# Hybrid decoder block on one core: attention weights scaled on GpSimd, compressed values in two heads at once, scan outputs parked in DRAM, one float32 product for each state

## The chip, the cores and the metric

The kernel runs on one core of a Trainium2 chip. Its engines are TensorE (PE: matmuls and transposes; PEld is its weight load), VectorE (DVE), ScalarE (ACT), GpSimd (POOL) and SyncE (SP, which issues all DMAs here). Each engine works through its own instructions in the order in which the program lists them and waits on semaphores for the others. The metric is device time in microseconds (us), median of several runs.

## The reference

One decoder layer over 1024 tokens of width 1024, in float32, cut here to what the change touches:

```python
h = rms_norm(x, norm1_w[l]) * (1.0 + sc1) + sh1
q, kv, nsa_g, z, xbc, dt_raw, mg = jnp.split(h @ w_in[l], IN_OFFSETS, axis=-1)
...
# sparse attention, 16 heads in 2 groups: compressed, selected and window branches
p_c = masked_softmax(s_c, cmp_end[None, :] <= t[:, None])      # 63 compressed keys
o_c = jnp.einsum('bgjtn,bngd->btgjd', p_c, v_cmp)
...
o = gb[..., 0:1] * o_c + gb[..., 1:2] * o_s + gb[..., 2:3] * o_w
...
# state-space scan, 4 groups of 8 heads, 8 chunks of 128 tokens in each
y_diag = jnp.einsum('bcgjls,bcsgjp->bclgjp', cb[:, :, :, None] * decay_in, xdt)
states = jnp.einsum('bcsgn,bcsgjp->bcgjpn', bm, xdt * decay_out[..., None])
y_off = jnp.einsum('bclgn,bcgjpn->bclgjp', cm, prev) * jnp.exp(a_cum)   # prev: state before the chunk
y = _rms(((y_diag + y_off) + d_skip * xs) * silu(z))             # by group
...
x = x + gt1 * ((g_attn * y_attn + g_ssm * y_ssm) @ w_o[l])
x = x + gt2 * ((silu(h2 @ w_gate[l]) * (h2 @ w_up[l])) @ w_down[l])
```

With 1024 tokens there are 16 blocks and 16 are selected, so the selected branch is causal attention over all keys.

## The kernel before

Most products are made of three: each float32 operand is split into a high part and the rest (`hi`, `lo`, in a format that TensorE takes at the rate of 512 columns in some 0.23 us), and hi·hi, hi·lo and lo·hi are added up (`mm3k`, lines 278 to 282). The split itself is ACT work (hi) and DVE or POOL work (lo; weights' lo is POOL's, L311).

The program is written out by a planner (`Flow`). Streams of TensorE work (Python generators) say what each step needs and how long it takes; four queues (A for ACT, V for DVE, G for POOL, D for DMA) hold the other work with a cost in us, which the planner multiplies by 1.15, 1.15, 1.2 and 1.0. It plays the streams against these costs and emits each instruction when it would start. So costs set the order in which each engine finds its work, and nothing else: on the chip each engine takes that order and waits where it must. Main streams go first; a filling stream (`background`) is put in where no main stream could go on, or as a credit allows that grows with `pace` times the main work.

Four stages follow each other. Projections (q, k, v, gates; the constants, cos and sin among them, lie in one tile `kc`). Attention: 32 units of 4 heads by 128 queries. For each of two branches, `score` makes S = qK (L1702), finds the row maximum on DVE (L1707), the exponential on ACT (L1711), and scales each head's P by 1/sum and its gate (L1720, DVE, four in a row). `value_step` turns P by 128 keys and 4 heads on TensorE (L1787), splits it (L1790 ACT, L1791 DVE) and `products` multiplies with V (L1018). The compressed branch has 64 keys: its turned P fills 64 partitions, and its two products have 64 rows. The filling stream here is the rest of the input projection (x, z and merge gates: `fps`), with the convolution on DVE (L1064, L1080), and `mod_rows` on POOL (L1276, L1279). Scan: 32 chunks; `prep` and `main` of `Chunk` make the diagonal part (yd), the part of the old state (yo), the norm and the new state (sp, st). In groups 0 and 1 yo and sp are single float32 products (L1922, L1949: two instructions each on TensorE); in groups 2 and 3 they are made in parts (`parts`, L1883 to L1888, and three products). `turn_y` turns each y for the output product, into tiles of the tag h32, of which there are three: two hold the attention's output until its product is done (`attn_done`), and one the first yT. The filling stream is the rest of the merge gates, the attention's output product (`aps`) and the scan's (`sps`). The last quarter of `sps` and the feed-forward layer are the tail, whose TensorE work stands without gaps.

## Time and profile before

| what | value |
|---|---|
| timed runs | 2707.79, 2699.96, 2702.74 us, median 2702.74 |
| the profiled execution | 2705.52 us, its span 2703.7 us |
| PE busy | 2581.8 us, 95% of the span |
| DVE, ACT, POOL busy | 1737.9, 1152.5, 664.0 us (64%, 43%, 25%) |
| mean granted TensorE clock | 0.977 |

A share of busy time is a mean over stages with different limits: PE is near full nearly everywhere, DVE is busiest in the attention and the scan, and nearly all of PE's idle time lies before the tail. The granted clock is given in shares of full speed (2.4 GHz); its lower level, 0.50, is 1.2 GHz. Times in a trace are counted from the span's start.

### The profile page before, as it was taken

How to read it: one execution, taken by the hardware profiler on the slowest of the kernel's cores; microseconds unless marked ns; L12 is line 12 of the kernel's file. 1: busy time of each engine (PE TensorE's matmuls, PEld its weight loads, DVE VectorE, ACT ScalarE, POOL GpSimd, SP SyncE). 2: the span in 40 equal slices, each digit the busy share in tenths (PEclk: the TensorE clock that was granted, in tenths of full speed). 3: DMA queues.
4: the chain of work that ended last, by engine and by line, in shares of the span. 5: the costliest groups of instructions: out<-in, count | busy, mean ns of one | idle time of the engine just before them, and what ended most of it. 6: DMA issues, size and time to landing. Idle time of an engine off the chain costs nothing.

```text
span 2703.7 us, 38173 instructions
## 1 busy us (share of the span) xinstructions
PE 2581.8 (95%) x14098; PEld 2185.0 (81%) x14098; DVE 1737.9 (64%) x4053; ACT 1152.5 (43%) x2458; POOL 664.0 (25%) x397
## 2 busy tenths in 40 slices
PE   6999999989998999999998999989999999999997
PEld 5999778878887888887877888769988888888885
DVE  7644987887886888877557579877722333333336
ACT  4322665556564655665545355542621111111113
POOL 2112222131222232312242322212122112222223
PEclk8999999999999999999998999989999999999999
DMA  6434232222223232212455544335221111111111
GB/s 234 142 105 143 85 86 63 64 78 71 63 67 126 86 92 73 90 43 71 138 164 190 188 139 129 106 122 171 73 77 40 39 47 47 47 47 47 47 55 63
DMA packets 206555, 253.95 MB, mean 94 GB/s; under 512 B 15256, under 2 KB 150040, under 8 KB 205856
## 3 DMA queue, kind: packets, MB, share of 16 engines
q1 hardware_dynamic: 206368, 251.51, 29.9%
q8 instruction: 111, 1.82, 0.3%
q14 instruction: 76, 0.62, 0.1%
HBM read 195.75 MB, written 55.71 MB: 93 GB/s over the span
## 4 chain that ended last, share of the span: by engine, by line
PE 79%; DVE 13%; DMA 3%; ACT 3%; issue 2%; SPq 0%; POOL 0%; DVEq 0%; ACTq 0%; POOLq 0%
PE fps L280 6%; PE gu L280 6%; PE fps L282 6%; PE fps L281 6%; PE gu L281 6%; PE gu L282 6%; PE o L1018 5%; PE tp L1787 4%; PE S L1702 4%; DVE P L1720 3%; PE dps L282 3%; PE dps L281 3%; PE dps L280 3%; PE yd L1905 2%; PE tokps L282 2%
## 5 line engine op out<-in xcount | busy, mean ns | idle before, releaser
L1569 DVE TENSOR_TENSOR x<-x,dps 128x512 f32<-128x512 f32 x176 | 120.9, 687 | 248.8 <-PE dps L282 248.6
L280 PE MATMUL gu<-m_hi,whi_w 128*128 128x512 f32 x704 | 279.8, 397 | 0.0
L281 PE MATMUL gu<-m_lo,whi_w 128*128 128x512 f32 x704 | 276.2, 392 | 0.0
L282 PE MATMUL gu<-m_hi,wlo_w 128*128 128x512 f32 x704 | 274.6, 390 | 0.0
L1790 ACT ACTIVATE kv<-tp 128x512 fp32r<-128x512 f32 (+1 forms) x296 | 172.9, 595 | 228.0 <-PE tp L1787 204.9
L311 POOL TENSOR_TENSOR wlo_w<-raw_w,whi_w 128x1024 fp32r<-128x1024 f32 x44 | 109.5, 2509 | 533.3 <-ACT whi_w L309 533.3
L1791 DVE TENSOR_TENSOR kv<-tp,kv 128x512 fp32r<-128x512 f32 (+1 forms) x296 | 196.7, 684 | 51.2 <-ACT kv L1790 50.0
L1018 PE MATMUL o<-kv 128*128 128x512 f32 x528 | 193.4, 420 | 12.5 <-DVE kv L1791 9.7
L1711 ACT ACTIVATE P<-P,sm 128x640 f32<-128x640 f32 (+7 forms) x256 | 186.5, 730 | 33.7 <-DVE sm L1707 32.4
L1702 PE MATMUL S<-kv,Q 128*128 128x384 f32 (+5 forms) x768 | 185.8, 344 | 6.7 <-DVE sm L1707 6.5
L1720 DVE TENSOR_SCALAR P<-P,sm,gate 128x640 f32<-128x640 f32 (+7 forms) x256 | 188.5, 800 | 1.2
L1787 PE MATMUL tp<-id,P 128*128 128x128 f32 x1056 | 157.9, 277 | 9.5 <-DVE Q L1666 5.9
L280 PE MATMUL fps<-hT_hi,whi_x 128*128 128x512 f32 x384 | 159.7, 416 | 4.0 <-ACT xs L1105 3.3
L282 PEld LDWEIGHTS gu<-m_hi,wlo_w 128*128 128x128 f32 x704 | 132.3, 188 | 33.0
L1787 PEld LDWEIGHTS tp<-id,P 128*128 128x128 f32 x1056 | 128.3, 142 | 37.5 <-issue 11.2
L280 PEld LDWEIGHTS gu<-m_hi,whi_w 128*128 128x128 f32 x704 | 132.1, 188 | 29.9
L281 PEld LDWEIGHTS gu<-m_lo,whi_w 128*128 128x128 f32 x704 | 131.8, 187 | 30.3
L282 PE MATMUL fps<-hT_hi,wlo_x 128*128 128x512 f32 x384 | 152.6, 397 | 0.0
L281 PE MATMUL fps<-hT_lo,whi_x 128*128 128x512 f32 x384 | 152.5, 397 | 0.0
L280 PE MATMUL fps<-whi_z,hT_hi 128*128 128x256 f32 x512 | 150.8, 295 | 0.9 <-ACT u L1067 0.6
L1702 PEld LDWEIGHTS S<-kv,Q 128*128 128x128 f32 x768 | 129.8, 194 | 24.0 <-DVE sm L1707 9.9
L1707 DVE CUSTOM_DVE_ANT_0 P<-S,kb 128x256 f32<-128x256 f32 (+5 forms) x256 | 120.5, 493 | 42.7 <-PE tp L1787 32.8
(342 smaller groups left out, 7046.7 us busy)
## 6 DMA issues: line engine op xcount, KB each, us to landing
wada<-w_ada SPq DMA_DIRECT2D x40, 512.0 KB, 4.3
ac<-acd SPq DMA_DIRECT2D x32, 512.0 KB, 4.9
raw_x<-w_in SPq DMA_DIRECT2D x24, 512.0 KB, 5.1
raw_w<-w_gate SPq DMA_DIRECT2D x22, 512.0 KB, 4.3
raw_w<-w_up SPq DMA_DIRECT2D x22, 512.0 KB, 3.8
rawd<-w_down SPq DMA_DIRECT2D x22, 512.0 KB, 3.8
xsd<-xs SPq DMA_DIRECT2D x32, 256.0 KB, 2.4
raw_z<-w_in SPq DMA_DIRECT2D x16, 512.0 KB, 4.7
```

Source lines behind the costliest of these rows:

```text
L280: mm(ps, lh, rh, start=k == 0, stop=False)
L281: mm(ps, lh, rl, start=False, stop=False)
L282: mm(ps, ll, rh, start=False, stop=k == kt - 1)
L1018: op = yield ([need, o], 0.22, lambda n=n, m=m, vst=vst, rows=rows, pair=pair: nc.tensor.matmul(o.t, vst(), pair()[m][:rows], start=n + m ...
L1569: e = V(0.6, [op], lambda ps=ps, t=t, cs=cs: nc.vector.tensor_tensor(self.x1[:, t, cs], self.x1[:, t, cs], ps.t, op=OP.add))
L1702: mm(sp[:, :w], q, kvb.kv[:, br, r, first + c0:first + c1], start=r == 0, stop=r == 1)
L1707: nc.vector.tensor_tensor_reduce(P[:, c0:c1], sp[:, :w], k.kb[:, m0:m0 + w], scale=-1.0, scalar=sm[:, 0, h:h + 1] if p else 3.0e38, op0=OP ...
L1711: ex = A(0.26 + 0.8333e-3 * n, [mx], lambda: nc.scalar.activation(P[:, :n], P[:, :n], AF.Exp, bias=sm[:, 1, h:h + 1], scale=-1.0, accum_ou ...
L1720: nc.vector.tensor_scalar(P[:, :n], P[:, :n], sm[:, 3, m:m + 1], k.gate[:, i, self.h0 + m, br + 1:br + 2], op0=OP.mult, op1=OP.mult)
L1787: nc.tensor.transpose(tp[:rows, h], P, k.id)
L1790: hi = A(0.48, [op, pair], lambda: nc.scalar.activation(pair()[0][:rows], tp[:rows], AF.Copy))
L1791: lo = V(0.6, [hi], lambda: nc.vector.tensor_sub(pair()[1][:rows], tp[:rows], pair()[0][:rows]))
```

## The change

Six things change.

- The scale of P (four for each branch of each unit, 256 in all) is issued on GpSimd instead of VectorE, with a cost of 0.25 + 1.08e-3 n.
- The compressed branch turns two heads at once (two transposes of 128 by 128 instead of four of 128 by 64), splits 128 by 256 instead of 64 by 512, and multiplies with values that stand twice, in the upper and the lower 64 partitions, with zeros between (`cvc`): four products of 128 rows and 256 columns instead of two of 64 rows and 512.
- In groups 2 and 3 of the scan the products with the state and for the state are single float32 ones as in groups 0 and 1; `parts` is gone.
- y of groups 1 and 2 is stored to DRAM by `main` and read back by `turn_y`; group 1 is not turned before `attn_done`.
- The pace of the scan's filling is 10 for 4.6 us of main work, in place of 16 in the first eight chunks and 5.6 after.
- The costs of the convolution are 2.5 and 0.75 instead of 2.25 and 0.66. cos, sin and one of the triangles move from `kc` to a tile `kt` in a buffer of the tag a1 that is given back after the projections.

```diff
@@ rope, load_constants, projections
-        cb = self.kc[:, K_COS + 8 * t:K_COS + 8 * t + 8][:, None, :].to_broadcast(sh)
+        cb = self.kt[:, 8 * t:8 * t + 8][:, None, :].to_broadcast(sh)
...
-        nc.sync.dma_start(self.kc, a["kc"][:, 0:K_ID])
+        nc.sync.dma_start(self.kc, a["kc"][:, 0:K_COS])
+        nc.sync.dma_start(self.kt.t, a["kc"][:, K_COS:K_ID])
...
+        self.kt = self.buf("a1", [128, K_ID - K_COS], "kt")
...
+        self.kt.until(*self.ktuse)
@@ products
-                vst, rows, pair, hi, lo = self.pv.pop(0)
-                for m, need in ((0, hi), (1, lo)):
-                    op = yield ([need, o], 0.22, lambda n=n, m=m, vst=vst, rows=rows, pair=pair: nc.tensor.matmul(
-                        o.t, vst(), pair()[m][:rows], start=n + m == 0, stop=n == u.total - 1 and m == 1))
+                vst, pair, hi, lo = self.pv.pop(0)
+                def product(m, n=n, vst=vst, pair=pair, o=o, u=u):
+                    if vst is None:
+                        for r in range(2):
+                            nc.tensor.matmul(o[:, r::2], self.cvc[:, u.g, r].rearrange("n r d -> n (r d)"),
+                                             pair()[m][:, 0:256], start=False, stop=False)
...
@@ background
-            c = V(2.25, [a0, a1, e], conv)
+            c = V(2.5, [a0, a1, e], conv)
...
-            f = V(0.66, [th], lambda: nc.vector.scalar_tensor_tensor(u.t, xr[:, 3:], 1.0, u.t, op0=OP.add, op1=OP.mult))
+            f = V(0.75, [th], lambda: nc.vector.scalar_tensor_tensor(u.t, xr[:, 3:], 1.0, u.t, op0=OP.add, op1=OP.mult))
@@ ssd, turn_y
-        pace = lambda: (16 if self.done < 8 else 5.6) / cost
+        pace = lambda: 10 / cost
...
-            while not self.ys:
+            while not self.ys or g == 1 and not self.attn_done:
                 yield None
             y, need = self.ys.pop(0)
+            if g in (1, 2):
+                y = self.buf("b", [128, 8, 64], f"yl{g}{c}")
+                need = D(0.73, [need, y], lambda y=y, g=g, c=c: nc.sync.dma_start(y.t.rearrange("p h d -> p (h d)"), self.yd[g - 1, c]))
@@ Unit.score
-                nc.vector.tensor_scalar(P[:, :n], P[:, :n], sm[:, 3, m:m + 1], k.gate[:, i, self.h0 + m, br + 1:br + 2],
+                nc.gpsimd.tensor_scalar(P[:, :n], P[:, :n], sm[:, 3, m:m + 1], k.gate[:, i, self.h0 + m, br + 1:br + 2],
                                         op0=OP.mult, op1=OP.mult)
-            self.P[br, m] = self.P[br, m][0], V(0.2 + 0.55e-3 * n, [e], scale)
+            self.P[br, m] = self.P[br, m][0], G(0.25 + 1.08e-3 * n, [e], scale)
@@ Unit.value_step
+        n = 2 if br == 2 else 4
+        c = slice(0, 128 * n)
...
+            for h in range(n):
+                P = self.P[2, 0][0][:, 2 * h:2 * h + 2].rearrange("p h n -> p (h n)") if br == 2 \
+                    else self.P[br, h][0][:, j * 128:(j + 1) * 128]
+                nc.tensor.transpose(tp[:, h * 128:h * 128 + 128], P, k.id)
@@ Chunk.main
-            if in_parts:
-                hi, lo, *es = self.parts("sp", lambda: self.bct[:, 1], self.l_bc, old, oldop)
...
+            op = yield ([oldop, yo], 0.86, lambda: nc.tensor.matmul(
+                fl(yo.t), self.bct[:, 1], fl(old.t), start=True, stop=True))
...
+        if self.g in (1, 2):
+            e = D(0.73, [e], lambda: nc.sync.dma_start(k.yd[self.g - 1, c], fl(y.t)))
+            y.until(e)
         k.ys.append((y, e))
```

Since the planner emits by costs, the order moves on every engine. Three places are shown. First DVE before, at the scale of the first branch of unit 2_0 of group 0 (P are its four heads, sm their sums; `ISA` is the row maximum):

```order
L1064 SCALAR_TENSOR_TENSOR u<-xr,hcw,u 128x512 x3
L1791 TENSOR_TENSOR kv_2828<-tp_1_1_3914,kv_2828 64x512
L1717 RECIPROCAL sm_2_0_3785<-sm_2_0_3785 128x4
L1665 TENSOR_TENSOR Q_2_1_3995<-tq_2_1_3960,Q_2_1_3995 64x256
L1666 TENSOR_TENSOR Q_2_1_3995<-tq_2_1_3960,Q_2_1_3995 64x256
L1080 SCALAR_TENSOR_TENSOR u<-xr,u 128x512
L1720 TENSOR_SCALAR P_2_0_3921<-P_2_0_3921,sm_2_0_3785,gate 128x384
L1720 TENSOR_SCALAR P_2_0_3949<-P_2_0_3949,sm_2_0_3785,gate 128x384
L1720 TENSOR_SCALAR P_2_0_3956<-P_2_0_3956,sm_2_0_3785,gate 128x384
L1720 TENSOR_SCALAR P_2_0_3968<-P_2_0_3968,sm_2_0_3785,gate 128x384
L1707 ISA P_2_0_4048,sm_2_0_3964<-S_2_0_3965,kb 128x384
```

And POOL now, at the same unit (wlo_x and wlo_z are weights' low parts for the filling, xr the convolution's input):

```order
L1762 TENSOR_SCALAR P_2_0_3793<-P_2_0_3793,sm_2_0_3718,gate 128x384
L1762 TENSOR_SCALAR P_2_0_3821<-P_2_0_3821,sm_2_0_3718,gate 128x384
L311 TENSOR_TENSOR wlo_x_3965<-raw_x_0_3907,whi_x_3939 128x1024
L1762 TENSOR_SCALAR P_2_0_3839<-P_2_0_3839,sm_2_0_3718,gate 128x384
L1762 TENSOR_SCALAR P_2_0_3849<-P_2_0_3849,sm_2_0_3718,gate 128x384
L311 TENSOR_TENSOR wlo_x_3965<-raw_x_4_3951,whi_x_3939 128x1024
L1108 MEMSET xr 128x3
L1762 TENSOR_SCALAR P_2_0_3953<-P_2_0_3953,sm_2_0_3852,gate 128x384
```

The four scales leave the row of convolution, splits and maxima on DVE and stand on POOL, in this unit with the low part of a weight tile between the second and the third.

Second, TensorE at the compressed step of the last unit, 7_1 of group 1 (Pc is its P, o the sum over keys, fps filling). Before:

```order
L1787 MATMUL tp_7_1_13668<-id,Pc_7_1_13519 64x128 x4
L280 MATMUL fps<-hT_hi,whi_m_13475 128x512
L281 MATMUL fps<-hT_lo,whi_m_13475 128x512
L282 MATMUL fps<-hT_hi,wlo_m_13491 128x512
L1018 MATMUL o_7_1_13557<-kv_8653 128x512
...
L1018 MATMUL o_7_1_13557<-kv_8653,cvc 128x512 x2
L1787 MATMUL tp_7_1_13687<-id,P_7_1_13450 128x128
```

Now:

```order
L1829 MATMUL tp_7_1_13672<-id,Pc_7_1_13518 128x128 x2
L1053 MATMUL o_7_1_13572<-kv_8506 128x512
...
L1050 MATMUL o_7_1_13572<-kv_8506,cvc 128x2x128 x2
L280 MATMUL fps<-hT_hi,whi_m_13516 128x512
L281 MATMUL fps<-hT_lo,whi_m_13516 128x512
L282 MATMUL fps<-hT_hi,wlo_m_13544 128x512
L1050 MATMUL o_7_1_13572<-kv_8506,cvc 128x2x128 x2
```

Two transposes stand where four stood, and two products of 256 columns for each one of 512. Over all 32 units the two products of before follow each other directly in 7 and are parted by other work in 25.

Third, TensorE where the scan ends. Before:

```order
L280 MATMUL yo_7_18199<-sph_7_18180 128x512
L281 MATMUL yo_7_18199<-spl_7_18190,sph_7_18180 128x512
L282 MATMUL yo_7_18199<-sph_7_18180,spl_7_18190 128x512
L1347 MATMUL yT_18216<-id,yy_6_18064 128x128 x4
L1347 MATMUL yT_18230<-id,yy_7_18183 128x128 x4
L280 MATMUL sps<-yT_17440,whi_so_17706 128x512
```

Now:

```order
L281 MATMUL sps<-yT_16986,whi_so_17450 128x512
L282 MATMUL sps<-yT_16986,wlo_so_17461 128x512
L1389 MATMUL yT_17837<-id,yy_7_17744 128x128 x4
L280 MATMUL sps<-yT_16986,whi_so_17450 128x512
```

Before, the last two y are turned side by side right after the last yo, and 96 rows of sps follow, the last quarter of them all, which needs those y. Now other sps stand on both sides, and 267 rows follow. Between the first and the last diagonal part there are 1371 rows of filling in the order before and 1179 now, each of 512 columns.

## Rows read from the trace of the kernel before

**Rows 1.** Busy time by stretch: attention, first part of the scan, its end, the tail. Columns: stretch and length in us, then PE, PEld, DVE, ACT, POOL busy (instructions), granted clock, DMA share, GB/s.

```profile
270.00:1335.00 1065.00, 1020.07 (x5959) 870.10 (x5958) 874.50 (x1952) 622.72 (x1435) 275.56 (x175) 0.98 0.26 79
1335.00:1493.00 158.00, 149.32 (x699) 119.83 (x698) 96.19 (x237) 78.43 (x167) 48.42 (x33) 0.96 0.58 184
...
1580.00:1830.00 250.00, 230.65 (x1130) 190.01 (x1130) 208.14 (x560) 135.83 (x320) 58.01 (x46) 0.93 0.39 121
1830.00:2704.00 874.00, 855.54 (x4088) 708.03 (x4086) 354.37 (x605) 191.16 (x289) 204.81 (x94) 1.00 0.20 62
```

**Rows 2.** Whom PE waited for in the attention, longest in total first: us in all, times, longest.

```profile
PE o L1018 <- DVE kv L1791: 10.0, 6, 5.6
PE S L1702 <- DVE sm L1707: 6.5, 4, 3.1
```

**Rows 3.** The longest of these waits: first the timeline of DVE, then of POOL, then of PE (start us, us, instruction, count, idle time before it), then the stretch behind the wait with its clock (columns as in rows 1).

```profile
596.68 5.77 DVE L1720 TENSOR_SCALAR P<-P,sm,gate 128x640 f32<-128x640 f32 x4
...
598.75 1.89 POOL L1276 TENSOR_TENSOR wada<-wada,sc 128x1024 f32<-128x1024 f32 x1 [0.83 <-DMA wada<-w_ada]
...
605.41 1.22 PE L1018 MATMUL o<-kv 128*128 128x512 f32 x2 [5.62 <-DVE kv L1791]
...
604.10:610.90 6.80, 5.49 (x20) 4.75 (x21) 5.49 (x13) 2.43 (x4) 4.34 (x4) 0.50 0.11 39
```

**Rows 4.** Costliest groups on DVE (from the page): busy us, mean ns of one.

```profile
L1720 DVE TENSOR_SCALAR P<-P,sm,gate 128x640 f32<-128x640 f32 (+7 forms) x256 | 188.5, 800 | 1.2
...
L1064 DVE SCALAR_TENSOR_TENSOR u<-xr,hcw,u 128x512 f32<-128x512 f32 x144 | 129.4, 898 | 11.7 <-ACT u L1067 7.9
```

**Rows 5.** Shortest, median and longest duration in ns of three DVE lines.

```profile
L1720 DVE TENSOR_SCALAR P<-P,sm,gate x256: 327/607/3009, 270.5 to 1307.8; 128x640 f32<-128x640 f32 x40, 128x128 f32<-128x128 f32 x16, 128x256 f32<-128x256 f32 x16, 128x384 f32<-128x384 f32 x16
...
L1064 DVE SCALAR_TENSOR_TENSOR u<-xr,hcw,u x144: 716/752/2872, 257.0 to 1124.8; 128x512 f32<-128x512 f32 x144
...
L1791 DVE TENSOR_TENSOR kv<-tp,kv x296: 659/684/693, 278.8 to 1332.2; 128x512 fp32r<-128x512 f32 x128, 64x512 fp32r<-64x512 f32 x20
```

**Rows 6.** POOL: groups in the attention (busy us, mean ns), and the durations of a product of two tiles of 128x512 in the scan.

```profile
L1279 POOL TENSOR_TENSOR acc<-acc,wada 128x512 f32<-128x512 f32 x64 | 89.9, 1405 | 3.6
...
L311 POOL TENSOR_TENSOR wlo_x<-raw_x,whi_x 128x1024 fp32r<-128x1024 f32 x20 | 49.7, 2501 | 158.7 <-ACT whi_x L309 149.1 <-PE fps L282 9.6
...
L1270 POOL MEMSET acc<- 128x512 f32 x8 | 4.2, 524 | 0.0
...
L1865 POOL TENSOR_TENSOR xw<-xs,etl x28: 1036/1044/1492, 1333.5 to 1780.9; 128x512 f32<-128x512 f32 x28
```

**Rows 7.** Timeline of PE at compressed steps (start us, us, instruction, count): the four transposes and what follows them; two products in a row; two products apart.

```profile
1204.80 0.60 PE L1787 MATMUL tp<-id,Pc 128*64 128x128 f32 x4
1205.15 0.48 PE L280 MATMUL fps<-hT_hi,whi_m 128*128 128x512 f32 x1
...
1208.40 0.73 PE L1018 MATMUL o<-kv,cvc 64*128 64x512 f32 x2
1209.07 0.66 PE L1787 MATMUL tp<-id,P 128*128 128x128 f32 x4
...
1244.23 0.50 PE L1018 MATMUL o<-kv,cvc 64*128 64x512 f32 x1
1244.66 0.66 PE L1787 MATMUL tp<-id,P 128*128 128x128 f32 x4
```

**Rows 8.** Timeline of PE in the projections: products of 128 rows and 256 columns.

```profile
200.05 0.28 PE L281 MATMUL tokps<-wlo_q,hT_hi 128*128 128x256 f32 x1
200.17 0.28 PE L282 MATMUL tokps<-whi_q,hT_lo 128*128 128x256 f32 x1
```

**Rows 9.** Timeline of PE in the scan: the product with the state as one float32 product (group 0), and in parts (group 2).

```profile
1376.80 1.02 PE L1922 MATMUL yo<-st,bct 128*128 128x512 f32 x2
1377.26 0.79 PE L280 MATMUL fps<-hT_hi,whi_m 128*128 128x512 f32 x1
1377.89 0.39 PE L281 MATMUL fps<-hT_lo,whi_m 128*128 128x512 f32 x1
...
1660.39 0.39 PE L280 MATMUL yo<-sph 128*128 128x512 f32 x1
...
1661.08 0.40 PE L280 MATMUL sps<-yT,whi_so 128*128 128x512 f32 x1
```

**Rows 10.** DVE in the end of the scan (1580 to 1830 us): the two wide low parts that groups 2 and 3 make (busy us, mean ns).

```profile
L1887 DVE TENSOR_TENSOR xpl<-xw,xph 128x512 fp32r<-128x512 f32 x14 | 9.5, 682 | 0.0
L1887 DVE TENSOR_TENSOR spl<-st,sph 128x512 fp32r<-128x512 f32 x14 | 9.5, 680 | 0.0
```

**Rows 11.** The last diagonal part and the last two turns of the scan on PE with the idle time before them, and the stretch around the turns with its clock (columns as in rows 1).

```profile
1811.88 1.89 PE L1905 MATMUL yd<-xs,E 128*128 128x64 f32 x16
...
1820.33 1.12 PE L1347 MATMUL yT<-id,yy 128*128 128x128 f32 x4 [3.75 <-ACT yy L1936]
1824.04 1.11 PE L1347 MATMUL yT<-id,yy 128*128 128x128 f32 x4 [2.60 <-ACT yy L1936]
...
1819.30:1829.50 10.20, 5.89 (x16) 4.07 (x17) 6.04 (x17) 3.96 (x8) 0.00 (x0) 0.50 0.19 69
```

**Rows 12.** Issues of DMA: KB each, median us from issue to landing, of a store and a load of 256 KB.

```profile
xsd<-xs SPq DMA_DIRECT2D x32, 256.0 KB, 2.4
...
xs<-xsd SPq DMA_DIRECT2D x32, 256.0 KB, 3.6
```

More of the change, by code (lines that the diff above doesn't have):

```diff
@@ L635, in q_evac @@
         r = V(1.65, [x, self.kcop], rot)
+        self.ktuse.append(r)
         d = D(0.7, [r], store)
@@ L943, in compress_part, with twice, high, low @@
         else:
+            h2 = self.buf("c7", [128, 2, 2, 2, 64], "hs2")
+            def twice():
+                for r in range(2):
+                    nc.vector.tensor_copy(h2[:, :, :, r], hs.t)
+            x = V(0.35, ev + [h2], twice)
             for g in range(2):
-                vp = self.buf("t", [64, 64], "vcp")
+                vp = self.buf("t", [128, 64], "vcp")
                 def mm(g=g, vp=vp):
                     for t in range(2):
-                        nc.tensor.matmul(vp.t, hs[:, t, g], w2[:, t], start=t == 0, stop=t == 1)
-                op = yield (ev + [c["d2"], vp], 0.22, mm)
-                y = A(0.11, [op], lambda g=g, vp=vp: nc.scalar.activation(self.cvc[:, g, 0], vp.t, AF.Copy))
-                self.cvcop = V(0.14, [y], lambda g=g, vp=vp: nc.vector.tensor_sub(self.cvc[:, g, 1], vp.t, self.cvc[:, g, 0]))
+                        nc.tensor.matmul(vp.t, h2[:, t, g].rearrange("p r n -> p (r n)"), w2[:, t], start=t == 0, stop=t == 1)
+                def high(g=g, vp=vp):
+                    for r in range(2):
+                        b = slice(64 * r, 64 * r + 64)
+                        nc.scalar.activation(self.cvc[b, g, r, 0], vp[b], AF.Copy)
+                def low(g=g, vp=vp):
+                    for r in range(2):
+                        b = slice(64 * r, 64 * r + 64)
+                        nc.vector.tensor_sub(self.cvc[b, g, r, 1], vp[b], self.cvc[b, g, r, 0])
+                op = yield ([x, c["d2"], vp], 0.22, mm)
+                y = A(0.46, [op, self.cvz], high)
+                self.cvcop = V(0.46, [y], low)
                 vp.until(self.cvcop)
+            h2.until(op)
             w2.until(op)
```

89 lines of the change are left out of this document (32 added, 57 removed).

## The prediction

> **What bounds the kernel now.** I read busy time by stretch first, then whom PE waited for, then the longest wait step by step, and last the durations of the instructions that the change touches.
>
> By stretch [rows 1], TensorE is the bound nearly everywhere, and what is not TensorE's work is in two places. In the attention (270 to 1335 us) PE is busy for 1020.07 of 1065 us, so 45 us are idle, and the granted clock is 0.98, which is worth another 0.02 x 1065 = 21 us. In the scan the two stretches with gaps have 8.7 and 19.4 us of idle time, and clocks of 0.96 and 0.93 (6.3 and 17.5 us): 28 + 24 = 52 us. The tail has a clock of 1.00, and the change does not reach it. So about 66 + 52 = 118 us could go at most, beside TensorE's own work.
>
> PE's waits in the attention are for DVE [rows 2], although DVE's mean load is only 874.5 of 1065 us, 82%. The longest shows why [rows 3]: four scales take 5.77 us on DVE where four medians of 0.607 us [rows 5] are 2.4. They end as a run of POOL's products ends (598.75 on); the low part L1791 behind them is late, PE sits idle for 5.62 us, and the clock behind it is at its lower level (0.50, 1.2 GHz) for 6.8 us, which costs 3.4 us more. The durations say the same of the whole: the scale has 327/607/3009 ns, the convolution 716/752/2872, but L1791, with one input in PSUM, 659/684/693 [rows 5]. The first two are held up by POOL, the last never. Blocked time is 256 x (800 - 607) = about 50 us for the scales and 144 x (898 - 752) = 21 us for the convolution [rows 4, 5].
>
> **Scale on POOL.** DVE loses 188.5 us [rows 4]. No scale on POOL is in the trace. A MEMSET of 128x512 takes 524 ns and reads nothing; a product of two tiles takes 1043 and reads two [rows 6]. So a scale of 512 lies between 0.52 and 1.04 us, and since it reads one tile I take the middle, 0.78. The mean width is 528 (4.5 tiles of 128 in one branch, 3.75 in the other), so 0.81 us each and 207 us in all, with ends of 138 and 275. POOL then has 276 + 207 = 483 of 1065 us, which is room enough, and four scales take 3.2 us, as on DVE now (4 x 0.80). P comes no later on average. The Trainium skill, "GPSIMD Engine Reference", 4.1 Engine selection, speaks against it: elementwise work belongs on VectorE, POOL being about 2x slower with two inputs, though about at line rate with one. By its 2x, 256 x 2 x 0.607 = 311 us, an estimate that POOL would still have room for; the product in rows 6 agrees (1043 against DVE's some 684).
>
> What stays blocked: the convolution, by a POOL that is busy for 483 instead of 276 us, 21 x 1.75 = 37 us. DVE has (874.5 - 188.5 + 16) / 1065 = 66% instead of 82%. Of the 66 us of waits and slow clock I keep the share of blocked time that is left, 37 of 71, and halve it, since DVE's free time, in which it catches up, grows from 18 to 34%: 66 x 0.52 x 0.53 = 18 us. PE's new waits for a P that POOL has late get 8 us. Gain: 66 - 26 = 40 us (bounds: 0 and 60; below nothing as a rival).
>
> **Compressed step.** Four transposes take 0.35 us from start to start of the next [rows 7], two are half: 32 x 0.175 = 5.6 us. Two products of 64 rows in a row take 0.67 us, one alone 0.43 [rows 7], where products of 128 rows and 256 columns start every 0.12 us [rows 8]. So 0.67 becomes 0.48 in 7 units, and 0.86 becomes 0.48 in 25: 1.3 + 9.5 = 10.8 us. Together 16 us of PE's own work, which nothing hides. The halved split (ACT, DVE) and the doubling of the hidden layer lie beside PE's filling and count for nothing.
>
> **One float32 product.** From 1376.80 the two instructions and the slow start behind them take 1.09 us until 1377.89, of which 0.23 is the next product's: 0.86 us. In parts it is 1660.39 to 1661.08, 0.69 us [rows 9]. So 28 x 0.17 = 5 us more on PE. In return DVE loses 9.5 + 9.5 us of wide low parts [rows 10], some 1.4 us a chunk, and the narrow ones.
>
> **Scan.** At its end PE waits 3.75 and 2.60 us for the last two norms, and the clock is at 0.50 for 10.2 us [rows 11]. Now other filling stands before those turns and 267 rows behind them instead of 96, so I count this as gone: 6.4 idle plus 5.1 for the clock, less what is counted twice, 10 us. The other 42 us I leave nearly as they are. The chunks come closer: 1179 rows of 0.23 us, and for each chunk 1.89 us of yd [rows 11], 0.35 for a turn as in rows 7, two products of 0.86 in seven of eight chunks and some 0.2 for cb, 3.9 in all, make 32 x 3.9 + 271 = 396 us, 12.4 a chunk. DVE now needs 208 us for 17 chunks [rows 1], 12.2, less some 1.6 for the parts, 10.6: 85% of 12.4, where it has 83% now. So DVE gains as much as it loses. y's way through DRAM, 2.4 + 3.6 us [rows 12], is far shorter than the time until its product, but its store waits in SP's queue for the norm, and the loads of the next chunks stand behind it; they are issued about two chunks (25 us) ahead. I take 12 us of gain (bounds: -25 and 40).
>
> kt's load stands where kc's stood in SP's queue and waits there for one of PE's first products; if the cover were gone it would cost the first rotations of k a few us once. The new costs change order alone. Both count as nothing.
>
> **Sum.** -16 + 5 - 40 - 12 = -63 us (-63.6 before rounding). The profiled execution took 2705.52, 2.8 us above the median of 2702.74, so the forecast is 2702.7 - 63.6 = 2639 us.
>
> **Rivals.**
> - The lock moves. What a scale did to itself it now does to others: POOL's scales, back to back, hold up the three steps of the convolution, and these hold up the scales, so that P is late on both sides. For it: 2872 ns in rows 5, with POOL busy for only a quarter of the stretch. Against: the pieces are 0.8 us instead of 2.5 us [rows 6]. The attention then gives 10 instead of 40: -16 + 5 - 10 - 12 = -33, 2669. The Trainium skill, "SBUF — State Buffer", Who interferes with whom, states it as a rule: a DVE instruction with two SBUF inputs and a reading GpSimd instruction exclude each other for the whole instruction, whoever is first. The trace agrees (rows 3 and 5).
> - The scan is too tight: 85% of DVE in one piece, with y's store ahead of loads in SP's queue, costs 25 us instead of giving 12: -16 + 5 - 40 + 25 = -26, 2676.
> - More goes: DVE at 66% has no long stalls, 60 us in the attention, 25 in the scan: -96, 2607.
> - Only TensorE's own work changes, because the planner trades the waits for others: -11, 2691.
> - Slower: POOL becomes the engine that PE waits for. If a scale costs what two inputs cost (2.04 ns an element), four of 640 columns take 5.2 us, 2 us longer than now, and a low part of 2.5 us [rows 6] can stand between them. Each such wait costs 2 us and about 3.4 us at half clock, 3.7. Of the 64 bursts, 40 are that wide or nearly; if half are late, that is 74 us more, and the attention's 40 do not come: 2702.7 - 16 + 5 - 12 + 74 = 2754. It decides from 7 late bursts on, where the -23 that are left are used up. Against it: POOL's idle half.
>
> **How the numbers follow.** Forecast 0.40, lock moves 0.17, scan too tight 0.13, more goes 0.15, only PE's work 0.06, slower 0.09. About 8 us (0.3%) is what a measurement of this kernel can tell from no change. The first four are faster beyond it, and most of the fifth: 0.86. Same 0.06. Slower 0.08, nearly all POOL. The range, 2600 to 2693, takes in all but the slower case and the lower half of "more goes".
>
> **What would show it.** Right: no DVE wait of PE over 3 us with a scale behind it; DVE near 700 us in the attention; POOL's scales near 0.8 us at 512 columns; steps of the compressed product every 0.12 us; no idle time at the last turns. Wrong: PE waiting for POOL's P in many units, convolution steps above 1 us on average, clock below 0.96 in the scan. The forecast falls if the scale costs over 1.3 us at its mean width, or if PE's idle time in the attention stays above 35 us.

## The result and the profile after

| what | before | after |
|---|---|---|
| median of the timed runs | 2702.89 us (2699.96 to 2707.79) | 2617.17 us (2613.43 to 2623.82) |
| the profiled execution, its span | 2705.52, 2703.7 us | 2613.43, 2611.7 us |
| PE, DVE, ACT, POOL busy | 95%, 64%, 43%, 25% | 97%, 60%, 43%, 34% |
| mean granted TensorE clock | 0.977 | 0.990 |

The changed kernel is faster: ratio 0.9684, 95% interval [0.9657, 0.9711]. That is 86 us where the forecast had 64; 2617 lies inside the range of 2600 to 2693.

Busy time by stretch of the changed kernel (columns as in [rows 1]): attention, scan, the filling behind the last turn, tail.

```profile
270.00:1269.00 999.00, 976.08 (x5968) 857.35 (x5968) 718.72 (x1707) 617.70 (x1433) 486.77 (x433) 1.00 0.28 84
1269.00:1700.00 431.00, 417.96 (x2045) 332.61 (x2044) 316.59 (x836) 223.78 (x503) 129.74 (x95) 0.98 0.56 180
1700.00:1760.00 60.00, 60.00 (x274) 50.00 (x273) 36.91 (x54) 12.14 (x19) 7.38 (x4) 1.00 0.49 160
1760.00:2612.00 852.00, 834.93 (x3986) 690.40 (x3984) 335.40 (x580) 185.57 (x281) 200.20 (x90) 0.99 0.19 58
```

The attention is 66 us shorter, and PE is idle for 22.9 us of it instead of 45. The stretches at the lower clock (0.50), half of whose length is lost, cost 3.4 us there where they cost 25.6. Scan and filling together took 515 us before and take 491. The tail has not moved.

Whom PE waited for in the attention, answering [rows 2] (us in all, times, longest):

```profile
PE o L1053 <- DVE kv L1833: 13.5, 10, 3.7
PE S L1744 <- DVE sm L1749: 3.4, 4, 1.3
PE o L1050 <- DVE kv L1833: 2.7, 3, 1.1
```

The waits are still for DVE, in smaller pieces; the wait of 5.6 us is gone. No wait of PE for the scale on POOL is in this list, although P is ready later than before: from the end of 1/sum to the end of the fourth scale it is 5.8 us on average over the 64 bursts, where it was 3.6 on DVE, since other work of POOL stands between the scales. The scale's durations, with those of the convolution and the low part (shortest, median, longest in ns, answering [rows 5]):

```profile
L1762 POOL TENSOR_SCALAR P<-P,sm,gate x256: 443/878/1545, 273.0 to 1245.1; 128x640 f32<-128x640 f32 x40, 128x128 f32<-128x128 f32 x16, 128x256 f32<-128x256 f32 x16, 128x384 f32<-128x384 f32 x16
...
L1101 DVE SCALAR_TENSOR_TENSOR u<-xr,hcw,u x144: 721/752/2934, 257.5 to 1098.1; 128x512 f32<-128x512 f32 x144
...
L1833 DVE TENSOR_TENSOR kv<-tp,kv x296: 406/685/693, 278.2 to 1266.0; 128x512 fp32r<-128x512 f32 x128, 128x256 fp32r<-128x256 f32 x20
```

In the groups of the page (busy us, mean ns) the scale has a mean of 855 ns, and the convolution is dearer than before, 991 instead of 898:

```profile
L1762 POOL TENSOR_SCALAR P<-P,sm,gate 128x640 f32<-128x640 f32 (+7 forms) x256 | 215.5, 855 | 374.5 <-DVE sm L1759 300.9
...
L1101 DVE SCALAR_TENSOR_TENSOR u<-xr,hcw,u 128x512 f32<-128x512 f32 x144 | 142.7, 991 | 16.3 <-ACT u L1104 11.3
```

Timeline of PE at a compressed step, where [rows 7] stood, then at the two products with the state in group 3, where [rows 9] stood, then at the last two turns, where [rows 11] stood (start us, us, instruction, count):

```profile
1253.03 0.38 PE L1829 MATMUL tp<-id,Pc 128*128 128x128 f32 x2
1253.16 0.48 PE L1053 MATMUL o<-kv 128*128 128x512 f32 x1
...
1254.39 0.40 PE L1050 MATMUL o<-kv,cvc 128*128 128x256 f32 x2
1254.63 0.39 PE L280 MATMUL fps<-hT_hi,whi_m 128*128 128x512 f32 x1
...
1605.08 1.02 PE L1939 MATMUL yo<-st,bct 128*128 128x512 f32 x2
1605.94 1.02 PE L1961 MATMUL sp<-xw,bdm 128*128 128x512 f32 x2
...
1694.55 0.60 PE L1389 MATMUL yT<-id,yy 128*128 128x128 f32 x4
1694.90 0.48 PE L280 MATMUL sps<-yT,whi_so 128*128 128x512 f32 x1
...
1697.07 0.60 PE L1389 MATMUL yT<-id,yy 128*128 128x128 f32 x4
1697.42 0.48 PE L280 MATMUL sps<-yT,whi_so 128*128 128x512 f32 x1
```

Two transposes take 0.13 us to the next start (four took 0.35), a pair of products 0.24 (one of 64 rows took 0.43), and a float32 product 0.86. At the last two turns PE no longer waits.

### The profile page after: what moved, and what is told of

Same layout as the page of the kernel before. It is cut to its first block, busy times and chain, and to the rows that moved or that the text cites. A ratio compares the mean times of both kernels' runs of the same rounds, so it can differ in the third digit from the quotient of the medians.

```text
span 2611.7 us, 38578 instructions
## 1 busy us (share of the span) xinstructions
PE 2528.2 (97%) x14070; PEld 2157.4 (83%) x14070; DVE 1568.1 (60%) x3745; ACT 1129.4 (43%) x2404; POOL 875.8 (34%) x654
## 5 line engine op out<-in xcount | busy, mean ns | idle before, releaser
L1762 POOL TENSOR_SCALAR P<-P,sm,gate 128x640 f32<-128x640 f32 (+7 forms) x256 | 215.5, 855 | 374.5 <-DVE sm L1759 300.9
L1833 DVE TENSOR_TENSOR kv<-tp,kv 128x512 fp32r<-128x512 f32 (+1 forms) x296 | 189.5, 657 | 116.0 <-ACT kv L1832 114.6
L1832 ACT ACTIVATE kv<-tp 128x512 fp32r<-128x512 f32 (+1 forms) x296 | 165.2, 574 | 190.8 <-PE tp L1829 184.3
L1579 DVE TENSOR_TENSOR sg<-sg,gu 128x512 f32<-128x512 f32 x44 | 30.3, 688 | 229.5 <-PE gu L282 229.5
L1573 ACT ACTIVATE sg<-gu 128x512 f32<-128x512 f32 x44 | 26.2, 596 | 292.0 <-PE gu L282 292.0
L1101 DVE SCALAR_TENSOR_TENSOR u<-xr,hcw,u 128x512 f32<-128x512 f32 x144 | 142.7, 991 | 16.3 <-ACT u L1104 11.3
```

Source lines behind the costliest of these rows:

```text
L1101: nc.vector.scalar_tensor_tensor(u.t, xr[:, k:k + N2], hcw[:, ft, k:k + 1], u.t, op0=OP.mult, op1=OP.add)
L1762: nc.gpsimd.tensor_scalar(P[:, :n], P[:, :n], sm[:, 3, m:m + 1], k.gate[:, i, self.h0 + m, br + 1:br + 2], op0=OP.mult, op1=OP.mult)
L1832: hi = A(0.064 + 0.104 * n, [op, pair], lambda: nc.scalar.activation(pair()[0][:, c], tp[:, c], AF.Copy))
L1833: lo = V(0.068 + 0.133 * n, [hi], lambda: nc.vector.tensor_sub(pair()[1][:, c], tp[:, c], pair()[0][:, c]))
```

## Experiments

Each kernel is compared with the kernel before on the same chip; its medians there were 2699.0, 2699.5 and 2700.4 us in the three groups of runs. The changed kernel has one group of its own, in which the kernel before took 2702.9 us; where a run is compared with the changed kernel, the difference of the medians is given, and by the ratios it would be 1 to 4 us larger. Two theories stand behind the attention's part. Lock: POOL's reading instructions hold up DVE's scales, and what is gained is that hold. Load: DVE is too full to catch up after any stall, and what is gained is the 190 us of work that it is rid of, whatever held it up.

**The scale alone** (on the kernel before).

```diff
-                nc.vector.tensor_scalar(P[:, :n], P[:, :n], sm[:, 3, m:m + 1], k.gate[:, i, self.h0 + m, br + 1:br + 2],
+                nc.gpsimd.tensor_scalar(P[:, :n], P[:, :n], sm[:, 3, m:m + 1], k.gate[:, i, self.h0 + m, br + 1:br + 2],
...
-            self.P[br, m] = self.P[br, m][0], V(0.2 + 0.55e-3 * n, [e], scale)
+            self.P[br, m] = self.P[br, m][0], G(0.25 + 1.08e-3 * n, [e], scale)
```

> The kernel before with the scale of P on GpSimd, nothing else. My theory: most of the gain of the whole change is the attention's, and the scale alone brings it; the attention loses some 50 of its 66 us of waits and slow clock, TensorE's own work stays: 2645 to 2660 us. Rival (the gain is spread over all parts): no more than 25 us, 2678 or later.

Measured: 2673.3 us, ratio 0.9902 [0.9887, 0.9917]: 26 us, between the two expectations. PE's idle time in the attention falls from 45 to 23.4 us, as in the whole change; its slow clock costs 13.7 us, between the 25.6 of before and the 3.4 of the whole change.

**The scale taken back** (from the changed kernel; the same edit reversed).

> The changed kernel with the scale of P back on VectorE at its old cost. My theory: the waits of the attention come back, some 50 us: 2660 to 2675 us, and PE's waits have blocked scales behind them again. Rival (spread): within 25 us of the changed kernel, 2642 at most.

Measured: 2659.4 us, ratio 0.9847 [0.9827, 0.9866], so without the scale on POOL the changed kernel is 42 us slower. That is just below my theory's range. The idle time in the attention is 49.2 us. PE's two largest waits in it (us in all, times, longest):

```profile
PE S L1744 <- DVE sm L1749: 14.7, 9, 3.1
PE o L1053 <- DVE kv L1833: 14.2, 10, 3.0
```

In front of nine of the ten late low parts (kv) DVE has a row of scales; the late maxima (sm) mostly stand behind steps of the convolution, and only one directly behind scales. This fits a DVE that the scale makes late as a whole, and not only in what follows it. Alone the scale is worth as much as the compressed step (26 and 27 us, below); the compressed step was not taken back from the changed kernel, so its worth on top of the rest is not known.

**Truer costs instead of another engine** (on the kernel before).

```diff
-            c = V(2.25, [a0, a1, e], conv)
+            c = V(2.5, [a0, a1, e], conv)
...
-            self.P[br, m] = self.P[br, m][0], V(0.2 + 0.55e-3 * n, [e], scale)
+            self.P[br, m] = self.P[br, m][0], V(0.44 + 0.56e-3 * n, [e], scale)
```

> The kernel before with costs that agree with what its trace shows: the scale 0.44 + 0.56e-3 n instead of 0.2 + 0.55e-3 n, the convolution 2.5 and 0.75; the scale stays on VectorE. Theory of the lock: single scales last up to 3 us and no mean cost foresees which; at most a third of the attention's 66 us goes, 2680 to 2703 us. Rival (the plan was only too tight on DVE): most of it goes, 2650 to 2665 us.

Measured: 2697.1 us, ratio 0.9995 [0.9982, 1.0008]. The planner then leaves DVE more room, by putting more filling into the attention, and nothing is gained in the whole. So truer costs for the same work are not what the change brings.

**The scale on DVE in the accumulating form** (on the kernel before; 1/sum and gate are multiplied first, and the sum that comes out is not used).

```diff
+        e = V(0.14, [e], lambda: nc.vector.tensor_tensor(sm[:, 3], sm[:, 3], k.gate[:, i, self.h0:self.h0 + 4, br + 1], op=OP.mult))
...
-                nc.vector.tensor_scalar(P[:, :n], P[:, :n], sm[:, 3, m:m + 1], k.gate[:, i, self.h0 + m, br + 1:br + 2],
-                                        op0=OP.mult, op1=OP.mult)
+                nc.vector.tensor_scalar(P[:, :n], P[:, :n], sm[:, 3, m:m + 1], 0.0, op0=OP.mult, op1=OP.add,
+                                        accum_out=sm[:, 0, m:m + 1])
...
-            self.P[br, m] = self.P[br, m][0], V(0.2 + 0.55e-3 * n, [e], scale)
+            self.P[br, m] = self.P[br, m][0], V(0.2 + 1.04e-3 * n, [e], scale)
```

> The kernel before with the scale still on VectorE, but in the form that also sums its result (the sum goes to a column that nobody reads; 1/sum and gate are multiplied first, one small instruction for four heads). It reads one tile at the plain rate, so it should take some 0.73 us at 640 columns, instead of 0.61 when free, but not be held up by GpSimd. Theory of the lock: no scale over 1.1 us, DVE as busy as before or less, and half or more of the attention's 66 us goes: 2650 to 2675 us. Rival (DVE's load is what counts): no gain, 2695 to 2715 us.

Measured: 2694.2 us, ratio 0.9983 [0.9974, 0.9993]. Durations of the scale (as in [rows 5]):

```profile
L1721 DVE TENSOR_SCALAR_CACHE_REDUCE P<-P,sm x256: 334/806/1279, 271.7 to 1385.3; 128x640 f32<-128x640 f32 x40, 128x128 f32<-128x128 f32 x16, 128x256 f32<-128x256 f32 x16, 128x384 f32<-128x384 f32 x16
L1721 DVE DVE_READ_ACCUMULATOR P<-P,sm x256: 75/82/87, 271.9 to 1386.1; 128x1 f32 x128
```

The hold is gone: the longest, 1279 ns, is one of 1024 columns, whose mean is 1274; before, the longest was 3009. But the median is 806 instead of 607 and 82 ns are read out behind each, so DVE's load is no lower. The gain is 5 us. The planner's cost of the scale was raised with the form, so the plan moved as well; against the kernel with truer costs (2697.1) it is 3 us. The Trainium skill, "SBUF — State Buffer", Who interferes with whom, excepts this form from the lock, and the trace agrees. The lock theory falls as I had put it: taking the hold off the scales, with DVE as loaded as before, gives next to nothing. That the hold counts through the load that it makes fits this, but is an inference.

**The scale on ScalarE** (on the changed kernel; factor made as above).

```diff
-                nc.gpsimd.tensor_scalar(P[:, :n], P[:, :n], sm[:, 3, m:m + 1], k.gate[:, i, self.h0 + m, br + 1:br + 2],
-                                        op0=OP.mult, op1=OP.mult)
+                nc.scalar.activation(P[:, :n], P[:, :n], AF.Copy, scale=sm[:, 3, m:m + 1])
...
-            self.P[br, m] = self.P[br, m][0], G(0.25 + 1.08e-3 * n, [e], scale)
+            self.P[br, m] = self.P[br, m][0], A(0.1 + 0.83e-3 * n, [e], scale)
```

> The changed kernel with the scale on ScalarE (one factor 1/sum x gate made beforehand on VectorE, 64 small products more). Theory of load (what counts is that VectorE is rid of 190 us, wherever they go): ScalarE has some 620 + 130 = 750 of 1000 us in the attention, which is room enough, and the time is 2605 to 2630. Theory of the lock (GpSimd's reads hold VectorE up, so a GpSimd with 276 instead of 487 us in the attention makes the convolution faster): below 2610, with the convolution's mean below 900 ns instead of 991. Rival (ScalarE's exponentials stand ahead of every scale and become the late step): 2640 or more, with TensorE waiting for P or for splits by ScalarE.

Measured: 2636.7 us, ratio 0.9769 [0.9745, 0.9794]: 20 us slower than on POOL, but 23 faster than on DVE, and outside all three ranges. The attention by engine (columns as in [rows 1]) and the scale's durations:

```profile
270.00:1286.00 1016.00, 982.86 (x5960) 860.61 (x5960) 729.06 (x1770) 764.59 (x1694) 277.89 (x177) 0.99 0.27 83
```

```profile
L1763 ACT ACTIVATE P<-P,sm x256: 386/770/1153, 275.8 to 1261.1; 128x640 f32<-128x640 f32 x40, 128x128 f32<-128x128 f32 x16, 128x256 f32<-128x256 f32 x16, 128x384 f32<-128x384 f32 x16
```

DVE is as free as in the changed kernel (729 against 719 us) and POOL as idle as before; the time still lies between. ACT is now the fullest at 75%, and PE waits for its high parts (4.4 us in 4 times, none in the changed kernel). The small product on DVE that makes the factor is a second cost of this form: its median is 164 ns, its longest 2165, and ACT waits for it 14 times (13.8 us). How the 20 us divide between the two is not settled. The convolution's mean is 984 ns although POOL is busy for 278 instead of 487 us, so what holds it up does not grow with POOL's load.

**One scale in four on ScalarE** (on the changed kernel).

```diff
...
+            self.P[br, m] = self.P[br, m][0], A(0.1 + 0.83e-3 * n, [e3], last) if m == 3 else G(0.25 + 1.08e-3 * n, [e], scale)
```

> The changed kernel with the scale of one head in four on ScalarE, the other three on GpSimd. GpSimd then has some 430 us instead of 487 in the attention and ScalarE some 665 instead of 620. If what is left of VectorE's waits is due to GpSimd's hold on it (34 us of the convolution's time are above its median), the convolution's mean falls below 950 ns and the time is 2606 to 2614. If TensorE's last 23 idle us are due to other things, or ScalarE's exponentials come later by as much: 2615 to 2626.

Measured: 2619.6 us, ratio 0.9698 [0.9681, 0.9714], no difference from the changed kernel, as the second expectation has it; the convolution has 1020 ns, not below 950.

**Idle load on DVE** (on the changed kernel).

```diff
+            def load():
+                for _ in range(4):
+                    nc.vector.reciprocal(k.pad, k.pad)
+
+            V(0.2 + 0.55e-3 * n, [e], load)
...
```

> The changed kernel, scales on GpSimd, with idle load put on VectorE where the scales stood: four reciprocals of a 128x4 tile of their own for each scale, whose results nothing uses, some 0.6 us each time and 150 us in all. They touch no P, no other engine waits for them, and they are too small to be held up by GpSimd for long. Theory of load (VectorE's share of the attention decides how late its low parts come): most of the 42 us that the scale on VectorE costs the changed kernel comes back, 2640 to 2660, with waits for kv above 20 us. Rival (what counts is P itself: it is made on another engine, so that the chain from the maximum to the turns is not behind the convolution): 2617 to 2628.

Measured: 2711.7 us, ratio 1.0042 [1.0026, 1.0058]: 95 us slower than the changed kernel, slower than the kernel before. POOL's scales begin 0.17 us behind the end of 1/sum, as without the load (median of 64 bursts in both traces), and the fourth ends 5.5 us behind it on average, 5.8 without the load; so P is not later. The attention (columns as in [rows 1]):

```profile
270.00:1366.00 1096.00, 1016.42 (x6000) 888.43 (x6000) 886.29 (x2732) 617.78 (x1433) 477.43 (x432) 0.96 0.25 76
```

DVE's share is 81% again, PE's idle time 79.6 us, what the slow clock costs 46 us, and every wait over 1.2 us is for DVE. One of 6.88 us, on the timelines of the engines (start us, us, instruction, count, idle time before it):

```profile
961.81 3.36 DVE L1771 RECIPROCAL pad<-pad 128x4 f32<-128x4 f32 x16
...
964.06 4.64 POOL L311 TENSOR_TENSOR wlo_x<-raw_x,whi_x 128x1024 fp32r<-128x1024 f32 x2
...
966.46 2.52 DVE L1799 TENSOR_TENSOR Pc<-Pc,st 128x256 f32<-128x256 f32 x1
968.90 0.55 DVE L1751 CUSTOM_DVE_ANT_0 P<-S,kb 128x384 f32<-128x384 f32 x1
...
969.51 1.01 PE L1746 MATMUL S<-kv,Q 128*128 128x384 f32 x2 [6.88 <-DVE sm L1751]
```

Sixteen small instructions delay DVE by 3.4 us; then a product of 128x256 with both inputs in SBUF takes 2.52 us (before, its line has a mean of 0.42), until just behind the end of POOL's pair of low parts (968.70); the row maximum behind it is late and PE stands. In this wait load and lock act together: the load takes the slack that otherwise swallows a hold. The holds themselves have not grown: what DVE's instructions in the attention take beyond the median of their kind is 71 us in all, 69 without the load and 104 in the kernel before. The load theory has the sign, but its size (2640 to 2660) was too small. Part of that is plain: a burst takes 3.4 us instead of the 2.4 that I had counted. The rest is not settled: with the scales themselves back on DVE its share is 84%, and that kernel is 52 us faster than this one, so the share alone does not give the time. No other run has DVE above 80% and POOL at 480 us at once.

**The compressed step alone** (on the kernel before; the hunks on `products`, `value_step`, `cvc` and `kt`).

> The kernel before with the compressed step alone changed (two heads turned at once, values standing twice, kt in its own tile); the scale of P stays on VectorE. The prediction's step says TensorE's own work falls by 16 us, which nothing hides: 2681 to 2692 with the kernel before at 2699 to 2703, and the products' starts 0.12 us apart. Rival (the waits for VectorE take up what TensorE gives back, as VectorE is as late as before): no difference beyond 4 us, 2695 to 2705. A second rival, from what is left over of the 86 us after the scale: the step gives 25 us or more, below 2678.

Measured: 2672.6 us, ratio 0.9895 [0.9861, 0.993]: 27 us, the second rival's side.

```profile
270.00:1301.00 1031.00, 985.28 (x5967) 863.68 (x5966) 869.05 (x1958) 614.16 (x1430) 281.09 (x176) 0.99 0.26 80
```

PE is idle as long as before (45.7 us), so this is PE's own work and the clock. In the profiled execution the attention is 34 us shorter. From the start of each compressed transpose and product to the start of the next instruction, added up over the attention, it is 13.3 + 26.2 us before and 5.2 + 16.4 now: 18 us. The stretches at half clock cost 13.7 us in this attention, 12 less than before. Some 4 us are found in neither.

**The scan as before** (changed kernel; pace, DRAM and parts undone).

> The changed kernel with the whole scan as before (parts in groups 2 and 3, old pace, no y in DRAM). The prediction's steps make the scan and the float32 product worth 7 us together: 2620 to 2629. From the two traces, in which the scan's waits and slow clock fell by 32 us and TensorE's work there rose by 7, it is 25 us: 2637 to 2650, with 25 us or more of idle time between the first diagonal part and the last turn. Rival (the scale sets free what the scan's filling needs, so the scan is as good with its old order): 2615 to 2620.

Measured: 2633.9 us, ratio 0.9759 [0.9731, 0.9786], between the two expectations; the new scan is worth 17 us on top of the rest. PE is idle for 30.9 us of the scan up to the last turn.

**The parts alone brought back** (changed kernel; `parts` in groups 2 and 3).

```diff
+            if in_parts:
+                hi, lo, *es = self.parts("sp", lambda: self.bct[:, 1], self.l_bc, old, oldop)
...
```

> The changed kernel with the products of groups 2 and 3 made in parts again; pace and y in DRAM stay as changed. The prediction's step says that TensorE saves 5 us and VectorE gets 1.4 us a chunk more work, and that the one is as large as the other: 2609 to 2620. Rival (the single product is what lets the scan run at the even pace, since it takes load and a step off the chain from the old state to the new): 2625 or more, with waits for VectorE's low parts in groups 2 and 3.

Measured: 2627.9 us, ratio 0.9734 [0.9709, 0.976], 11 us slower than the changed kernel: the rival. PE's idle time up to the last turn is 26.6 us instead of 13.0; only 2.4 us of it are waits for the low parts themselves, the rest is spread over loads, norms and turns. The wait for a norm at a turn (`yT` for `yy`) is down to 0.5 us here, where the old scan has 11.7: with pace and DRAM as changed the last norms are covered with parts too, but the time goes into other waits, 6.4 us for loads (`bct`) and 4.7 of a filling product for DVE (`rq`) the largest.

**The single product without the rest of the new scan.**

```diff
-        pace = lambda: 10 / cost
+        pace = lambda: (16 if self.done < 8 else 5.6) / cost
...
-            while not self.ys or g == 1 and not self.attn_done:
+            while not self.ys:
...
-            if g in (1, 2):
-                y = self.buf("b", [128, 8, 64], f"yl{g}{c}")
...
-        if self.g in (1, 2):
-            e = D(0.73, [e], lambda: nc.sync.dma_start(k.yd[self.g - 1, c], fl(y.t)))
```

> The changed kernel with the old pace of the scan and without y in DRAM; the single float32 products of groups 2 and 3 stay. With the whole old scan the changed kernel took 2633.9, with parts alone 2627.9. Theory: the single product takes a low part and its ScalarE copy off the chain from the old state to the new, and that is most of the scan's gain whatever the pace: 2619 to 2627. Rival (it pays only together with the even pace, which keeps TensorE filled while VectorE catches up): 2630 to 2637, with the waits for the last norms of 11 us as in the kernel before.

Measured: 2617.15 us, ratio 0.9692 [0.9675, 0.971]: the time of the changed kernel, and just below my theory's range. This kernel and that with the old scan differ in the single product alone. First the old scan: its stretch (columns as in [rows 1]), PE's waits in it (us in all, times, longest), the filling in it (count | busy us, mean ns | idle), and the last two turns.

```profile
1264.00:1755.00 491.00, 460.13 (x2240) 374.31 (x2239) 350.00 (x916) 250.13 (x569) 131.30 (x95) 0.96 0.47 151
```

```profile
PE yT L1384 <- ACT yy L1973: 11.7, 5, 3.7
...
PE sp L281 <- DVE xpl L1924: 4.0, 2, 2.7
PE yo L281 <- DVE spl L1924: 2.6, 2, 1.9
```

```profile
L280 PE MATMUL sps<-yT,whi_so 128*128 128x512 f32 x226 | 95.9, 424 | 1.2 <-ACT yT L1388 0.7 <-DVE yacc L1294 0.5
```

```profile
1748.79 0.66 PE L1384 MATMUL yT<-id,yy 128*128 128x128 f32 x4 [3.75 <-ACT yy L1973]
1752.05 1.12 PE L1384 MATMUL yT<-id,yy 128*128 128x128 f32 x4 [2.60 <-ACT yy L1973]
```

Now the old pace, no DRAM, and the single product:

```profile
1264.00:1700.00 436.00, 415.88 (x2042) 329.92 (x2041) 317.48 (x836) 224.91 (x503) 130.44 (x95) 0.99 0.50 158
```

```profile
PE yT L1386 <- ACT yy L1950: 1.8, 3, 1.4
```

```profile
L280 PE MATMUL sps<-yT,whi_so 128*128 128x512 f32 x170 | 78.8, 464 | 4.9 <-DVE rq L252 2.3 <-DVE yacc L1294 1.1 <-ACT yacc L1292 0.8
```

```profile
1697.57 0.39 PE L282 MATMUL sps<-yT,wlo_so 128*128 128x512 f32 x1
1697.80 0.60 PE L1386 MATMUL yT<-id,yy 128*128 128x128 f32 x4
```

With the single product the planner uses up 56 triples of filling fewer in the scan, 56 x 3 x 0.227 = 38 us, and they stand behind the last turn instead, where they cover the last norms. The waits for norms fall from 11.7 to 1.8 us, those for low parts (4.0 + 2.6) are gone with the parts, and the clock rises from 0.96 to 0.99. DVE has 317 us of work instead of 350.

DVE's share does not explain it. Here are groups 2 and 3 alone, from their first diagonal part to the last turn (columns as in [rows 1]), with the old scan and with the single product:

```profile
1523.00:1753.00 230.00, 211.71 (x1048) 175.20 (x1047) 191.06 (x512) 125.18 (x294) 53.83 (x42) 0.94 0.38 121
1522.00:1699.00 177.00, 169.15 (x856) 131.81 (x855) 159.01 (x433) 101.86 (x232) 52.86 (x42) 1.00 0.42 131
```

DVE is at 83% in the first and at 90% in the second, and yet PE is idle for 18 us in the first and 8 in the second. In the changed kernel the same stretch has 73% (165 of 225 us) and 4 us. What the single product takes away is the split by ACT and DVE in front of the products, and 32 us of DVE's work with it; the two were not tried apart.

**The new scan alone** (on the kernel before).

> The kernel before with the new scan alone (single products, even pace, y in DRAM); attention, scale and compressed step as before. If the parts of the change add up, this is 17 us faster than before, as the scan is on top of the other two parts: 2678 to 2688. Rival (the new scan needs an attention that ends with less filling left over or less load): 2692 or more. By the prediction's steps it would be 7 us, 2690 to 2696.

Measured: 2683.7 us, ratio 0.9937 [0.992, 0.9955], 17 us, as adding up has it: within the intervals the scan's part does not depend on the others.

**The attention of these runs side by side** (from busy time by stretch, us from 270 to its end; idle is length less PE busy; slow clock is half the length of the stretches at 0.50). The three runs not listed change the scan alone; their attention is that of the kernel they start from, within 5 us.

| kernel | length | PE idle | slow clock | DVE busy (share) | POOL busy | time of the whole |
|---|---|---|---|---|---|---|
| before | 1065 | 45 | 26 | 875 (82%) | 276 | 2702.9 |
| + scale on POOL | 1029 | 23 | 14 | 732 (71%) | 484 | 2673.3 |
| + compressed step | 1031 | 46 | 14 | 869 (84%) | 281 | 2672.6 |
| + truer costs (more filling inside) | 1112 | 41 | 9 | 881 (79%) | 295 | 2697.1 |
| + accumulating form (more filling inside) | 1125 | 36 | 14 | 911 (81%) | 292 | 2694.2 |
| changed, old scan | 994 | 21 | 0 | 717 (72%) | 488 | 2633.9 |
| changed, scale on DVE | 1039 | 49 | 15 | 869 (84%) | 279 | 2659.4 |
| changed, scale on ACT | 1016 | 33 | 10 | 729 (72%) | 278 | 2636.7 |
| changed, one in four on ACT | 1000 | 25 | 3 | 746 (75%) | 440 | 2619.6 |
| changed, idle load on DVE | 1096 | 80 | 46 | 886 (81%) | 477 | 2711.7 |
| changed | 999 | 23 | 3 | 719 (72%) | 487 | 2617.2 |

## Why the prediction was right, and where it was not

- **Scale on POOL, -40.** Right in its sizes: 855 ns instead of 810, POOL 487 us instead of 483, DVE 72% instead of 66%. In the profiled executions the scale alone takes the attention's idle time and slow clock from 71 to 37 us (44.9 + 25.6 to 23.4 + 13.7), and undoing it puts 38 back on 26: 33 and 38 where 40 were forecast. (The whole change takes off 44; the other 11 are clock, as in the kernel with the compressed step alone.) As a part of the time it is 26 us alone and 42 when undone.
- **The working behind the scale.** It was half right. Blocked time was the wrong measure: the accumulating form takes the hold off the scales and gains 5 us. The other half, DVE's free time in which it catches up, is what the table bears out in the main (71 to 75% goes with 21 to 43 us of idle time and slow clock, 79 to 84% with 49 to 126), and the idle load shows how dear its loss is; but equal shares stand beside quite different times, so the share is no measure of its own. The forecast that POOL's busier hours would block the convolution for 21 x 1.75 = 37 us came near (142.7 - 144 x 0.752 = 34), but that was luck, as the rule is wrong: with the scale on ACT and POOL at 278 us it is 33, and with only the costs changed, on DVE and with POOL at 295, it is 47. "P comes no later on average" was wrong as well (5.8 us behind 1/sum instead of 3.6), and the 8 us for it were not needed: PE did not wait. Two readings do not hold as they stand: 1043 ns against 684 is 1.5 times and not 2 (the scale itself has 878 against 607, 1.45); and the hold in rows 3 is on a scale, which reads one tile, so of these rows only the convolution's in rows 5 bear on a rule for two inputs.
- **Compressed step, -16.** The mechanism was right, and the direct term nearly so: 18 us from start to start. Alone it gave 27 us (19 to 38 by the interval). In the profiled execution the clock gives another 12 us, which the sum did not have; why the clock is better there was not tried by itself.
- **One float32 product, +5.** PE's cost was nearly right: by the traces of before and after, PE's work at full clock from the start of the scan to the end of its filling is some 462 us with parts and 469 with the single product, 7 us more. The sign of the whole was wrong: it is 11 us faster than parts at the new pace, 17 at the old. The step that failed is "DVE gains as much as it loses", which compared DVE's shares of a chunk in groups 2 and 3, 83% and 85%. Measured they are 83% before, 90% with the single product at the old pace and 73% in the changed kernel, and the last two kernels take the same time; so the share is not what decides. What went was the way through ACT and DVE before the products, with its waits, and the filling that the planner had put there and that was then missing at the end.
- **Scan, -12.** The last turns came as forecast (no idle time, 267 rows behind them). I gave that to pace and DRAM, which do cover the norms (0.5 us of waits with parts), but so does the single product without them (1.8 us). For the time, pace and DRAM bring nothing with the single product (2617.15 against 2617.17), and 6 us with parts, within the intervals. The rest of the scan's waits and slow clock, which I left "nearly as they are", went for the most part too: idle time and slow clock in scan and filling fell from 52 to 20 us. The 1371 and 1179 rows of filling are those up to the last turn; up to the last diagonal part the traces have 1362 and 1110. A chunk took 13.1 us where the working had 12.4. Scan and product together are 17 us where the sum had 12 - 5 = 7.
- **kt and the costs, 0.** The convolution's costs, with a truer one for the scale, are 0 (ratio 0.9995); kt's load was not tried alone.
- **The sum.** 22 us are missing from it: some 11 from the compressed step and 10 from scan and product, if the scale is given its 40 (it has 26 alone and 42 undone). The ratios of the three parts alone multiply to 0.9902 x 0.9895 x 0.9937 = 0.9736, the whole is 0.9684: 14 us more than the parts. With their intervals added as independent this is about as wide as its uncertainty, so whether scale and compressed step help each other stays open. The two profiled executions are 92 us apart, 6 more than the medians, so terms read from them add up to too much.
- **Rivals.** The lock did move: the convolution is held for 34 us instead of 21, and its mean of 991 ns is just under the 1 us that was to be a sign of being wrong. It did not cost what that rival said, and the changed kernel has DVE at 72%. The scan was not too tight. The slower case needed PE to wait for P; it never did, and even with DVE loaded up the waits were for DVE. The result lies between the forecast and "more goes" (2607): waits and clock gave 44 us in the attention of the profiled pair, where the two had 40 and 60, and 32 in the scan, where they had 12 and 25, less the 7 us of the product.

## What to carry to other kernels

An engine at 82% that feeds TensorE can be on the path: look at the share it has in the stage and at whom TensorE waits for, and try to move work to an engine at a quarter even if each instruction gets longer there; then ask whether the engine that takes it is still free (here POOL at 49% was, ACT at 75% made TensorE wait). The share alone decides nothing: in the last two groups of the scan DVE ran at 90% and TensorE hardly waited. Before crediting a new order of the work, run the old order with the other edits. The cost of a step on the bounding engine said little here, where the dearer step takes two other engines out of a chain that the planner had covered with filling it needed later.

## What the runs showed of the hardware that was not expected

- DVE's scale of P in the accumulating form was never held up as the plain one was (longest 1279 instead of 3009 ns), but is slower when free (median 806 instead of 607).
- ACT's scale has a median of 770 ns over the same 256 tiles, POOL's 878, DVE's 607: three engines within a factor of 1.5.
- A product of 64 rows and 512 columns has a median of 0.42 us to the start of a next instruction of 128 rows (57 times) and 0.34 to another of 64 rows (7 times), where one of 128 rows and 512 columns takes 0.23.
- Sixteen reciprocals of 128x4 take 3.36 us on DVE, 0.21 us each, so small instructions are no small load.
- The convolution's steps have means of 984, 1020 and 991 ns with POOL busy for 278, 440 and 487 us of the attention, and of 898 to 1078 in kernels that have POOL at 276 to 295 us, the highest with only the planner's costs changed (its median is 752 in all): how long POOL is busy does not tell how long it holds them up.
